# Low parts and masking on GpSimd, wider value products and a bf16 sum in a hybrid attention layer

## The chip, the cores and the metric

The kernel runs on one core of one Trainium2 chip. The metric is the device time of one launch in microseconds (us). Five engines work side by side, each in the order of its own instructions: TensorE (PE, with its weight loads as PEld), VectorE (DVE), ScalarE (ACT), GpSimd (POOL) and SyncE (SP), which issues most DMAs.

## The reference

One decoder layer on x of 2048 rows by 1024 columns. The rows are normalised and modulated, one projection gives the inputs of two attentions of 8 heads of 64 each, both are gated, put side by side, projected again, normalised and added to x. The change lies in the first attention (A), the "forgetting" one, with a causal mask and a bias from a cumulative sum `cum` of log gates:

```python
s = jnp.einsum('bhqd,bhkd->bhqk', qb, kh, preferred_element_type=jnp.float32) * scale
s = s + cb[..., None] - cum[:, :, None, :]
causal = key_pos[None, :] <= q_pos[:, None]
s = jnp.where(causal, s, -jnp.inf)
p = jax.nn.softmax(s, axis=-1)
return jnp.einsum('bhqk,bhkd->bhqd', p.astype(vh.dtype), vh)
...
y = jnp.concatenate([oa, ob], axis=-1) @ w_out[l]
x = x + gate[:, None, :] * rms_norm(y, g_post[l])
```

All of it is in float32.

## The kernel before

float32 products are made of float16 ones: each operand is split into a high part (rounded to float16) and a low part (what is left), and high x high, high x low and low x high are summed in PSUM.

After a start and the second attention (to about 460 us) comes attention A, 8 heads of 20 steps. A step (`Step`, L1331) holds two blocks of 128 keys (b) against a chunk of 512 queries (ci); u is the block of 128 queries in the chunk. `scores` (L1341) makes the scores transposed, keys on partitions, in one two-bank PSUM tile `st`: two products a block (L1349, L1350), of 512, 384, 256 or 128 columns, since blocks above the diagonal are left out. For the 4 blocks on the diagonal of each chunk a third product adds the mask, an identity times a bf16 matrix of -1e30 (L1352). A step is thus 1024, 896 or 384 columns wide; the last two are the diagonal ones. `exp32` (L1354) takes the exponential on ACT into float32 `p32`; `high` (L1358) rounds it to float16 on ACT; `low` (L1362) subtracts on DVE. `pv` (L1365) multiplies with the values: for each key block and u it runs three products with their own weight loads (L1373 high x (64 high value columns and a column of ones), L1375 high x 64 low value columns, L1376 low x 65), all into 65 columns a u of one PSUM tile `po`. The column of ones gives the softmax denominator. After the last step of a chunk DVE takes the reciprocal (L1380) and one product (L1382) into `ona`, and `o_store` (L283) splits and stores it: the high part on ACT, the low part on DVE (L291), DMAs on SP. `po` has one buffer, so the next chunk's first product waits for L1382. `p32` and `ph` have three.

The order is written out by hand in one loop over the steps (L1671). In step s: `exp32(s)`; delayed actions (`tick`); `low(s-1)`; half of the step's other work; `high(s)`; `scores(s+1)`; `tick`; `pv(s-2)`; the other half. The other work is what fills PE: units of three products of the next heads' projections (L351), and products for the row maxima (L1300), each followed on DVE by a maximum (L1303 or L1305) that frees its PSUM bank. `rows` (L1308) turns maxima into limbs by small DVE instructions (L1317 to L1320). Weights for later heads are loaded by POOL (`w_load`, L221), their largest element goes out and back through HBM (L230, L235), and they are split (L267, L273); gate products are stored by POOL (L394) after DVE's product (L392). The gate of the output is summed on DVE (`gate_use`, L1237), and the output weights are split in the last two heads (L1443).

The output projection follows, 16 tiles of 128 rows (`Out`, L1462), begun in the last head. Each tile is scaled by a power of two near the root of its sum of squares: ACT sums each partition (L1510), PE adds over partitions by a float32 product with a matrix of ones (`scale_`, L1514).

Of the kernel before, what the change touches and what calls it, by code (L numbers as in the profile page):

```python
# [24 lines left out]
CH = 512  # L25
# [4 lines left out]
NEG = -1.0e30  # L30
# [5 lines left out]
XM, XR, VW = 66, 69, 129  # L36
# [7 lines left out]
def hybrid_layer(  # L44
# [17 lines left out]
    V, A, G, PE, SP = nc.vector, nc.scalar, nc.gpsimd, nc.tensor, nc.sync  # L62
# [12 lines left out]
    const = ctx.enter_context(tc.tile_pool(name="const", bufs=1))  # L75
# [7 lines left out]
    def sm(n, tag):  # L83
        return small.tile([P, n], F32, tag=tag, name=tag)
# [69 lines left out]
    Shp = const.tile([P, KT], F32, name="Shp")  # L154

    ident = const.tile([P, P], F32, name="ident")
    identb = const.tile([P, P], BF16, name="identb")
    identh = const.tile([P, P], F16, name="identh")
    dmaskT = const.tile([P, P], BF16, name="dmaskT")
    lift = const.tile([P, 1], F32, name="lift")  # L160
    pfl = const.tile([P, 1], F32, name="pfl")
    csum = const.tile([P, 8, NB], F32, name="csum")
# [2 lines left out]
    ones = const.tile([P, P], F32, name="ones")  # L165
# [297 lines left out]
    start = ExitStack()  # L463
    st = start.enter_context(tc.tile_pool(name="start", bufs=1, reuse_waits="tile"))
    wad = start.enter_context(tc.tile_pool(name="wad", bufs=8, reuse_waits="tile"))
    with tc.manual_schedule():
# [23 lines left out]
            w_load(key, pieces(key))  # L490
        G.dma_start(snk[:], sinks[0].partition_broadcast(P))
        G.dma_start(bfg[:], b_fgate[0].partition_broadcast(P))
        V.tensor_copy(identb[:], ident[:])
        V.tensor_copy(identh[:], ident[:])
        PE.transpose(bk[0][:, :P], rows[:], ident[:])
        cols = st.tile([P, 40], F32, name="cols")
# [41 lines left out]
        zero = st.tile([P, P], F32, name="zero")  # L538
# [4 lines left out]
        dm32t = st.tile([P, P], F32, name="dm32t")  # L543

        G.affine_select(dm32t[:], zero[:], [[1, P]], ALU.is_ge, NEG, base=0, channel_multiplier=-1)

        G.affine_select(triu[:], ones[:], [[1, P]], ALU.is_ge, 0.0, base=0, channel_multiplier=-1)

# [33 lines left out]
        A.activation(dmaskT[:], dm32t[:], AF.Copy)  # L582

        def col8(name):
            return st.tile([P, KT], F32, name=name)
# [745 lines left out]
    class Step:  # L1331
# [9 lines left out]
        def scores(self):  # L1341
            T, ci = Ts[self.hd % 2], self.ci
            self.st = ps_st.tile([P, 2 * CH], F32, tag="st", name="sta")
            for b, u0, o in self.blocks:
                w = CH - u0 * P
                kb_ = slice(b * P, (b + 1) * P)
                qc = slice(ci * CH + u0 * P, (ci + 1) * CH)
                diag = b >= 4 * ci
                PE.matmul(self.st[:, o:o + w], T[:, 3, kb_], T[:, 1, qc], start=True, stop=False)  # L1349
                PE.matmul(self.st[:, o:o + w], T[0:XR, 2, kb_], T[0:XR, 0, qc], start=False, stop=not diag)  # L1350
                if diag:
                    PE.matmul(self.st[:, o:o + P], identb[:], dmaskT[:], start=False, stop=True)  # L1352

        def exp32(self):  # L1354
            self.p32 = fxp.tile([P, 2 * CH], F32, tag="p32", name="p32")
            A.activation(self.p32[:, :self.w], self.st[:, :self.w], AF.Exp, scale=scl[f"qk{self.hd}"][:], bias=lift[:])  # L1356

        def high(self):  # L1358
            self.ph = fxh.tile([P, 2, 2 * CH], F16, tag="ph", name="pha")
            A.activation(self.ph[:, 0, :self.w], self.p32[:, :self.w], AF.Copy)  # L1360

        def low(self):  # L1362
            V.tensor_tensor(self.ph[:, 1, :self.w], self.p32[:, :self.w], self.ph[:, 0, :self.w], op=ALU.subtract)  # L1363

        def pv(self):  # L1365
            hd, ph = self.hd, self.ph
            if self.first:
                self.po_[0] = ps_po.tile([P, 4, 65], F32, tag="po", name="poa")
            po = self.po_[0]
            for n, (b, u0, o) in enumerate(self.blocks):  # L1370
                for u in range(u0, 4):
                    pq = slice(o + (u - u0) * P, o + (u - u0 + 1) * P)
                    PE.matmul(po[:, u, :], ph[:, 0, pq], vt[:, b, hd, 0:65],  # L1373
                              start=(self.first and n == 0 and u == 0), stop=False)
                    PE.matmul(po[:, u, 0:64], ph[:, 0, pq], vt[:, b, hd, 65:VW], start=False, stop=False)  # L1375
                    PE.matmul(po[:, u, :], ph[:, 1, pq], vt[:, b, hd, 0:65], start=False,  # L1376
                              stop=(self.last and n == len(self.blocks) - 1))
            if self.last:
                rinv = sm(4, "a_ri")
                V.reciprocal(rinv[:], po[:, :, 64])  # L1380
                on = op_.tile([P, 4, 64], F32, tag="ona", name="ona")
                V.tensor_tensor(on[:], po[:, :, 0:64], rinv[:].unsqueeze(2).broadcast_to([P, 4, 64]), op=ALU.mult)  # L1382
# [79 lines left out]
    class Out:  # L1462
# [24 lines left out]
        def turn(self, lag):  # L1487
# [6 lines left out]
            self.sc = sm(1, "w_pw")  # L1494
            hi, lo = self.hl[:, 0], self.hl[:, 1]
            gs = sm(1, "w_mx")

            def gate():
                if self.t < 4:
# [11 lines left out]

            def scale_():
                pg = bk[bank()][:, 0:1]
                PE.matmul(pg, ones[:], gs[:], start=True, stop=True)  # L1514
# [269 lines left out]
```

## Time and profile before

| | |
|---|---|
| time, median of 3 runs | 1157.74 us (1156.0 to 1158.17) |
| time of the profiled execution | 1157.8 us |
| its span, first to last instruction | 1156.1 us |
| PE busy | 1116.8 us (97%) |
| DVE busy | 930.5 us (80%) |
| ACT busy | 661.4 us (57%) |
| POOL busy | 207.5 us (18%) |
| mean granted PE clock | 0.996 |

How to read it: a row of a group gives line, engine, operation, what it writes and reads, shape and count, then the busy time in us and the mean in ns of one, then the idle time of the engine just before these instructions and what ended it. A row of the timeline gives start and length in us, engine, line and operation. A row of waits gives who waited, for whom, the total in us, the times and the longest. Matmuls overlap in PE's pipe, so their lengths add up to more than their time.

### The profile page before, as it was taken

The numbers are of one execution on the slowest core, as the hardware profiler recorded it, in microseconds if no ns is written. First come the engines' busy times: TensorE is split into PE (matmuls) and PEld (weight loads), VectorE is DVE, ScalarE is ACT, GpSimd is POOL, SyncE is SP. The second block draws the span as 40 slices with busy tenths as digits, with TensorE's granted clock in tenths as the row PEclk, the third lists the DMA queues.
The fourth block names the chain that finished last, engine by engine and source line by source line (L and its number), as shares of the span: only waits on it lengthen the run. The fifth ranks groups of instructions, "written<-read, shape, count | busy, mean of one in ns | idle before, by whom it ended". The sixth has DMA issues, their size and how long they took to land. (4 is left out here: it accounts for less than half of the span.)

```text
span 1156.1 us, 25291 instructions
## 1 busy us (share of the span) xinstructions
PE 1116.8 (97%) x9869; PEld 656.3 (57%) x9869; DVE 930.5 (80%) x2137; ACT 661.4 (57%) x1150; POOL 207.5 (18%) x332
## 2 busy tenths in 40 slices
PE   5899999999999999999999999999999999999997
PEld 2475544577765866555555555555555555544444
DVE  7877468987888568788988899888888887878885
ACT  2876344654555421666757666666776778534332
POOL 1122134554556530010010110001000000000000
PEclk9899999999999999999999999999999999999999
DMA  9943355433243232442344342123311337686743
GB/s 333 336 116 72 87 78 96 97 63 90 52 92 88 58 87 58 73 108 29 80 64 87 84 67 70 38 49 76 45 43 34 91 101 206 140 225 197 199 135 109
DMA packets 123476, 120.10 MB, mean 104 GB/s; under 512 B 64948, under 2 KB 100828, under 8 KB 123356
## 3 DMA queue, kind: packets, MB, share of 16 engines
q1 hardware_dynamic: 112088, 85.69, 27.6%
q0 software_dynamic: 10832, 32.50, 13.5%
q8 instruction: 77, 1.26, 0.6%
q14 instruction: 43, 0.35, 0.1%
q10 hardware_dynamic: 436, 0.28, 0.1%
HBM read 64.75 MB, written 25.18 MB: 78 GB/s over the span
## 5 line engine op out<-in xcount | busy, mean ns | idle before, releaser
L1356 ACT ACTIVATE p<-sta,lift,scl_qk 128x1024 f32<-128x1024 f32 (+2 forms) x160 | 172.0, 1075 | 131.6 <-PE sta L1350 82.6
L351 PE MATMUL bk<-hT,wh_qk 128*128 128x512 f16 x768 | 194.7, 378 | 0.0
L1363 DVE TENSOR_TENSOR pha<-p,pha 128x1024 f16<-128x1024 f32 (+2 forms) x160 | 169.1, 1057 | 0.2 <-ACT pha L1360 0.2
L1303 DVE TENSOR_REDUCE a_m<-bk 128x1 f32<-128x512 f32 x192 | 130.4, 686 | 45.8 <-PE bk L1300 44.8
L1576 PE MATMUL bk<-wohl,oz 128*128 128x512 f16 x744 | 165.3, 379 | 1.1 <-DVE oz L1525 0.7
L1360 ACT ACTIVATE pha<-p 128x1024 f16<-128x1024 f32 (+2 forms) x160 | 148.1, 926 | 5.9 <-PE poa L1376 1.2
L1576 PEld LDWEIGHTS <-oz 128*128 128x128 f16 x744 | 71.9, 99 | 82.8 <-DVE oz L1525 1.8
L1376 PE MATMUL poa<-vt,pha 128*128 128x65 f16 x1088 | 116.1, 192 | 1.4 <-DVE pha L1363 1.2
L1373 PE MATMUL poa<-vt,pha 128*128 128x65 f16 x1088 | 116.6, 193 | 0.8 <-DVE ona L1382 0.7
L1375 PE MATMUL poa<-vt,pha 128*128 128x64 f16 x1088 | 116.6, 194 | 0.0
L351 PEld LDWEIGHTS <-wh_qk 128*128 128x128 f16 x768 | 72.1, 97 | 74.4 <-issue 2.1
L1349 PE MATMUL sta<-T 128*128 128x512 f16 (+1 forms) x320 | 110.9, 346 | 2.8 <-ACT p L1356 2.7
L1300 PE MATMUL bk<-T 66*128 66x512 f16 (+2 forms) x320 | 109.7, 348 | 2.4 <-DVE a_m L1303 1.9
L1373 PEld LDWEIGHTS <-pha 128*128 128x128 f16 x1088 | 101.5, 96 | 15.5 <-DVE ona L1382 1.9
L1350 PE MATMUL sta<-T 69*128 69x512 f16 (+1 forms) x320 | 109.8, 348 | 0.0
L1375 PEld LDWEIGHTS <-pha 128*128 128x128 f16 x1088 | 100.9, 97 | 11.4
L1376 PEld LDWEIGHTS <-pha 128*128 128x128 f16 x1088 | 100.8, 99 | 1.8 <-DVE pha L1363 1.7
L351 PE MATMUL bk<-hT,wh_za 128*128 128x512 f16 x384 | 99.7, 378 | 0.0
L369 PE MATMUL bk<-wh_va,hT 128*128 128x256 f16 x768 | 91.9, 273 | 0.0
L351 PE MATMUL bk<-hT,wh_zb 128*128 128x512 f16 x384 | 91.6, 379 | 0.2 <-DVE qc L754 0.2
L351 PE MATMUL bk<-hT,wh_qb 128*128 128x512 f16 x384 | 91.2, 379 | 0.0
L369 PEld LDWEIGHTS <-hT 128*128 128x128 f16 x768 | 73.3, 98 | 12.2 <-issue 2.1
(459 smaller groups left out, 1919.7 us busy)
## 6 DMA issues: line engine op xcount, KB each, us to landing
hT<-in_x_dram SPq DMA_DIRECT2D x20, 512.0 KB
wa<-in_w_ada_dram SPq DMA_DIRECT2D x16, 512.0 KB
z_d<-tz POOLq DMA_DIRECT2D x32, 256.0 KB, 3.0
T<-z_d SPq DMA_DIRECT2D x16, 512.0 KB
T<-stq SPq DMA_DIRECT2D x62, 128.0 KB
out_dram<-hT SPq DMA_DIRECT2D x15, 512.0 KB
xt<-in_x_dram SPq DMA_DIRECT2D x12, 512.0 KB
qs<-qf SPq DMA_DIRECT2D x80, 64.0 KB
```

Of the source, the lines that this page charges most:

```text
L351: PE.matmul(ps, whl[:, a, k, :], hT[ci][:, b, k, :], start=(k == 0 and n == 0), stop=(k == KT - 1 and n == 2))
L369: PE.matmul(ps[:, (u % 2) * 2 * P:(u % 2 + 1) * 2 * P], hT[ci][:, a, k, u * P:(u + 1) * P], wv[p][:, b, k, :], start=(k == 0 and n == 0), ...
L1303: V.tensor_reduce(m3[:, u, pc:pc + 1], mx[:, :w], axis=AX.X, op=ALU.max)
L1349: PE.matmul(self.st[:, o:o + w], T[:, 3, kb_], T[:, 1, qc], start=True, stop=False)
L1350: PE.matmul(self.st[:, o:o + w], T[0:XR, 2, kb_], T[0:XR, 0, qc], start=False, stop=not diag)
L1356: A.activation(self.p32[:, :self.w], self.st[:, :self.w], AF.Exp, scale=scl[f"qk{self.hd}"][:], bias=lift[:])
L1360: A.activation(self.ph[:, 0, :self.w], self.p32[:, :self.w], AF.Copy)
L1363: V.tensor_tensor(self.ph[:, 1, :self.w], self.p32[:, :self.w], self.ph[:, 0, :self.w], op=ALU.subtract)
L1373: PE.matmul(po[:, u, :], ph[:, 0, pq], vt[:, b, hd, 0:65], start=(self.first and n == 0 and u == 0), stop=False)
L1375: PE.matmul(po[:, u, 0:64], ph[:, 0, pq], vt[:, b, hd, 65:VW], start=False, stop=False)
L1376: PE.matmul(po[:, u, :], ph[:, 1, pq], vt[:, b, hd, 0:65], start=False, stop=(self.last and n == len(self.blocks) - 1))
L1576: PE.matmul(py, self.hl[:, i, k, :], w_slot(8 * j + k)[:, cc], start=(k == 0 and m_ == 0), stop=(k == KT - 1 and m_ == 2))
```

## The change

Four things change in attention A and one in the output projection.

- The mask products and their constants go. Where a step's blocks are diagonal, POOL zeroes the masked part of `p32` after the exponential (an `affine_select` in place over the first 128 columns of both blocks). `high` and `low` read `p32` after it.
- `low` runs on POOL.
- For u below 3 the two products with the high part become one of 129 columns, (64 high values, ones, 64 low values). For u = 3 there is no room in the bank, and the three products stay.
- The evacuation adds the two halves: a reciprocal, a copy, a sum, a product for u = 3, and a product from SBUF.
- The sum of the tiles' squares takes the upper 16 bits of both operands as bfloat16.

```diff
                 PE.matmul(self.st[:, o:o + w], T[:, 3, kb_], T[:, 1, qc], start=True, stop=False)
-                PE.matmul(self.st[:, o:o + w], T[0:XR, 2, kb_], T[0:XR, 0, qc], start=False, stop=not diag)
-                if diag:
-                    PE.matmul(self.st[:, o:o + P], identb[:], dmaskT[:], start=False, stop=True)
+                PE.matmul(self.st[:, o:o + w], T[0:XR, 2, kb_], T[0:XR, 0, qc], start=False, stop=True)
...
             A.activation(self.p32[:, :self.w], self.st[:, :self.w], AF.Exp, scale=scl[f"qk{self.hd}"][:], bias=lift[:])
+            b, u0, o = self.blocks[1]
+            if b >= 4 * self.ci:
+                d = self.p32[:, 0:2 * o].rearrange("p (a c) -> p a c", a=2)[:, :, 0:P]
+                G.affine_select(d, d, [[0, 2], [1, P]], ALU.is_ge, 0.0, base=0, channel_multiplier=-1)
...
-            V.tensor_tensor(self.ph[:, 1, :self.w], self.p32[:, :self.w], self.ph[:, 0, :self.w], op=ALU.subtract)
+            G.tensor_tensor(self.ph[:, 1, :self.w], self.p32[:, :self.w], self.ph[:, 0, :self.w], op=ALU.subtract)
...
-                self.po_[0] = ps_po.tile([P, 4, 65], F32, tag="po", name="poa")
-            po = self.po_[0]
+                self.po_[0] = ps_po.tile([P, CH], F32, tag="po", name="poa")
+            whole = self.po_[0]
+            po = [whole[:, VW * u:VW * u + (VW if u < 3 else 65)] for u in range(4)]
...
-                    PE.matmul(po[:, u, :], ph[:, 0, pq], vt[:, b, hd, 0:65],
+                    PE.matmul(po[u], ph[:, 0, pq], vt[:, b, hd, 0:VW if u < 3 else 65],
                               start=(self.first and n == 0 and u == 0), stop=False)
-                    PE.matmul(po[:, u, 0:64], ph[:, 0, pq], vt[:, b, hd, 65:VW], start=False, stop=False)
-                    PE.matmul(po[:, u, :], ph[:, 1, pq], vt[:, b, hd, 0:65], start=False,
+                    if u == 3:
+                        PE.matmul(po[u][:, 0:64], ph[:, 0, pq], vt[:, b, hd, 65:VW], start=False, stop=False)
+                    PE.matmul(po[u][:, 0:65], ph[:, 1, pq], vt[:, b, hd, 0:65], start=False,
...
-                V.reciprocal(rinv[:], po[:, :, 64])
+                V.reciprocal(rinv[:], whole[:, 64:3 * VW + 65:VW])
                 on = op_.tile([P, 4, 64], F32, tag="ona", name="ona")
-                V.tensor_tensor(on[:], po[:, :, 0:64], rinv[:].unsqueeze(2).broadcast_to([P, 4, 64]), op=ALU.mult)
+                p3 = whole[:, 0:3 * VW].rearrange("p (u c) -> p u c", u=3)
+                V.tensor_copy(on[:, 0:3], p3[:, :, 65:VW])
+                V.tensor_tensor(on[:, 0:3], p3[:, :, 0:64], on[:, 0:3], op=ALU.add)
+                V.tensor_scalar(on[:, 3], po[3][:, 0:64], rinv[:, 3:4], None, op0=ALU.mult)
+                V.tensor_tensor(on[:, 0:3], on[:, 0:3], rinv[:, 0:3].unsqueeze(2).broadcast_to([P, 3, 64]), op=ALU.mult)
...
+            gs1 = gs[:].bitcast(BF16)[:, 1:2]
...
-                PE.matmul(pg, ones[:], gs[:], start=True, stop=True)
+                PE.matmul(pg, ones[:].bitcast(BF16).rearrange("p (n two) -> p two n", two=2)[:, 1], gs1,
+                          start=True, stop=True)
```

At the start the bf16 identity (a copy on DVE), the transposed mask (a select on POOL) and its conversion to bf16 (on ACT) go. Line numbers of the changed kernel differ from those of before by up to 11.

POOL in attention A before, in the second head (gw are the gate rows, wr the raw weights, mx_d and mxr the largest elements out and back, z_d the gate products):

```order
L394 DMA z_d<-tz 128x512
L1231 DMA gw_6936<-in_w_ada_dram 128x1024
L394 DMA z_d<-tz 128x512
L221 DMA wr_qk_7244<-in_w_in_dram 128x8x64 x2
L221 DMA wr_za_7312<-in_w_in_dram 128x8x128
```

The same stretch's beginning in the changed kernel (L1350 is the zeroing, L1357 the low part, p is `p32`):

```order
L392 DMA z_d<-tz 128x512
L1357 TENSOR_TENSOR pha<-p_6760,pha 128x1024
L1357 TENSOR_TENSOR pha<-p_6805,pha 128x1024
L1224 DMA gw_6900<-in_w_ada_dram 128x1024
L1357 TENSOR_TENSOR pha<-p_6858,pha 128x1024
L1350 AFFINE_SELECT p_6949<-p_6949 128x2x128
L1357 TENSOR_TENSOR pha<-p_6902,pha 128x1024
L1350 AFFINE_SELECT p_7005<-p_7005 128x2x128
L1357 TENSOR_TENSOR pha<-p_6949,pha 128x896
```

Between two DMA issues now stand low parts, and a step's zeroing stands ahead of the low part of the step before it. A low part stands behind a store that waits for DVE.

PE before, where the scores of a diagonal step end and value products begin (T are the stacked queries and keys):

```order
L1350 MATMUL sta<-T_6056 128x384
L1352 LDWEIGHTS identb
L1352 MATMUL sta<-dmaskT,identb 128x128
L1373 LDWEIGHTS pha
L1373 MATMUL poa<-vt,pha 128x65
L1375 LDWEIGHTS pha
L1375 MATMUL poa<-vt,pha 128x64
L1376 LDWEIGHTS pha
L1376 MATMUL poa<-vt,pha 128x65
```

And such a place in the changed kernel:

```order
L1342 MATMUL sta<-T_6047 128x384
L1368 LDWEIGHTS pha
L1368 MATMUL poa<-vt,pha 128x129
L1372 LDWEIGHTS pha
L1372 MATMUL poa<-vt,pha 128x65
```

The mask product with its weight load is gone, and two of the three weight loads and products remain.

DVE at the end of a chunk, before (a_ri is the reciprocal, a_m are maxima):

```order
L1363 TENSOR_TENSOR pha<-p_7799,pha 128x1024
L1305 ISA bk_136,a_m<-bk_136,cmask 128x128
L1305 ISA a_m 128x1
L1380 RECIPROCAL a_ri<-poa 128x4
L1382 TENSOR_TENSOR ona<-poa,a_ri 128x256
L1303 TENSOR_REDUCE a_m<-bk_138 128x1
```

And in the changed kernel:

```order
L1376 RECIPROCAL a_ri<-poa 128x4
L1379 COPY ona<-poa 128x192
L1380 TENSOR_TENSOR ona<-poa,ona 128x192
L1381 TENSOR_SCALAR ona<-poa,a_ri 128x64
L1382 TENSOR_TENSOR ona<-ona,a_ri 128x192
```

The low part is no longer ahead of the evacuation; of its five instructions four read the bank, and the last reads SBUF alone.

More of the change, by code (lines that the diff above doesn't have):

```diff
@@ L156, in hybrid_layer @@
     ident = const.tile([P, P], F32, name="ident")
-    identb = const.tile([P, P], BF16, name="identb")
     identh = const.tile([P, P], F16, name="identh")
-    dmaskT = const.tile([P, P], BF16, name="dmaskT")
     lift = const.tile([P, 1], F32, name="lift")
@@ L492, in hybrid_layer @@
         G.dma_start(bfg[:], b_fgate[0].partition_broadcast(P))
-        V.tensor_copy(identb[:], ident[:])
         V.tensor_copy(identh[:], ident[:])
@@ L542, in hybrid_layer @@
         G.affine_select(dm32[:], zero[:], [[-1, P]], ALU.is_ge, NEG, base=0, channel_multiplier=1)
-        dm32t = st.tile([P, P], F32, name="dm32t")
-        G.affine_select(dm32t[:], zero[:], [[1, P]], ALU.is_ge, NEG, base=0, channel_multiplier=-1)
         G.affine_select(triu[:], ones[:], [[1, P]], ALU.is_ge, 0.0, base=0, channel_multiplier=-1)
@@ L581, in hybrid_layer @@
         A.activation(dmask[:], dm32[:], AF.Copy)
-        A.activation(dmaskT[:], dm32t[:], AF.Copy)
         def col8(name):
@@ L1347, in scores @@
                 qc = slice(ci * CH + u0 * P, (ci + 1) * CH)
-                diag = b >= 4 * ci
                 PE.matmul(self.st[:, o:o + w], T[:, 3, kb_], T[:, 1, qc], start=True, stop=False)
-                PE.matmul(self.st[:, o:o + w], T[0:XR, 2, kb_], T[0:XR, 0, qc], start=False, stop=not diag)
-                if diag:
-                    PE.matmul(self.st[:, o:o + P], identb[:], dmaskT[:], start=False, stop=True)
+                PE.matmul(self.st[:, o:o + w], T[0:XR, 2, kb_], T[0:XR, 0, qc], start=False, stop=True)
         def exp32(self):
```

## The prediction

> **What bounds the kernel now.** I read the page's totals first, then the busy time by stretch, then the timeline of TensorE.
>
> ```profile
> span 1156.1 us, 25291 instructions
> PE 1116.8 (97%) x9869; PEld 656.3 (57%) x9869; DVE 930.5 (80%) x2137; ACT 661.4 (57%) x1150; POOL 207.5 (18%) x332
> 462.00:1001.00 539.00, 530.96 (x5503) 309.34 (x5502) 465.76 (x1011) 380.13 (x465) 35.55 (x57) 1.00 0.34 76
> 1001.00:1156.00 155.00, 147.09 (x725) 71.10 (x723) 119.01 (x304) 51.95 (x98) 0.00 (x0) 0.99 0.63 175
> ```
>
> The first line is the span; around it lie 1.7 us, since the profiled execution took 1157.8 us, which is the median of the runs to within 0.1 us. The last two rows give length, then the busy time of PE, PEld, DVE, ACT and POOL, the granted clock, and DMA. The causal attention runs from 462 to 1001 us; nearly all of the change lies there. PE is busy for 531 of its 539 us at full clock; behind it only the output projection is left, where PE is full again. DVE, at 466 of 539, is next; POOL is almost free. So a nanosecond taken from PE comes out of the time, and work taken off DVE does not, unless DVE makes PE wait. A busy figure for PE overlaps in its pipe, so I price products by the distance from one start to the next:
>
> ```profile
> 562.34 0.19 PE L1373 MATMUL poa<-vt,pha 128*128 128x65 f16 x1
> ...
> 563.05 0.19 PE L1376 MATMUL poa<-vt,pha 128*128 128x65 f16 x1
> 563.08 0.38 PE L351 MATMUL bk<-hT,wh_za 128*128 128x512 f16 x1
> ...
> 614.17 0.22 PE L1352 MATMUL sta<-dmaskT,identb 128*128 128x128 bf16 x1
> 614.23 0.19 PE L1373 MATMUL poa<-vt,pha 128*128 128x65 f16 x1
> 614.26 0.19 PE L1375 MATMUL poa<-vt,pha 128*128 128x64 f16 x1
> 614.29 0.19 PE L1376 MATMUL poa<-vt,pha 128*128 128x65 f16 x1
> ...
> 83.70 0.87 PE L795 MATMUL bk<-wh_vb,hT 128*128 128x136 f16 x12
> 84.41 0.81 PE L351 MATMUL bk<-hT,wh_zb 128*128 128x512 f16 x3
> ...
> 1045.11 0.28 PE L1514 MATMUL bk<-w_mx,ones 128*128 128x1 f32 x2
> 1045.25 0.59 PE L1576 MATMUL bk<-wohl,oz 128*128 128x512 f16 x2
> ```
>
> Between 562.34 and 563.08 stand 24 value products of 64 or 65 columns, 30.8 ns each, every one with its own weights. Twelve products of 136 columns take 0.71 us, 59 ns each. A mask product of 128 columns takes 60 ns, a product of the tiles' squares (two passes) 140 ns. PE's pace thus goes by columns, not by instructions.
>
> **Value products.** Of the 1088 triples (65, 64, 65 columns), the 768 with query block u below 3 become a pair (129 and 65). A triple costs 3 x 30.8 = 92.5 ns, a pair 59 (the 136-column row) + 30.8 = 89.8 ns: 768 x 2.7 ns = **2.1 us less**. The ends: nothing, if 129 columns cost twice 30.8 ns; 23.7 us, if a product's price did not depend on its columns, which the 136-column row rules out.
>
> The Trainium skill, "TensorE: Matmul & The Clock Gate", section "Back-to-back issue gap", says that a stream of weight load and product pairs is spaced at about 81 ns for 128 columns. This trace has 59 and 60 ns in such streams, so it disagrees; the rule stays as a rival below, since it would turn the merge into a loss.
>
> **Mask products.** 128 go (L1352), at 60 ns: **7.7 us less**. **Squares:** 16 times 140 ns become one pass of a column, at most one small product (30.8 ns): 16 x 0.11 = **1.8 us less**. At the start a select like L547's below (0.3 us) and two conversions go too; PE waits for its weights to land there, so I cost them at nothing:
>
> ```profile
> PE pm L514 <- DMA wa<-in_w_ada_dram: 4.9, 3, 2.0
> ```
>
> **Low parts.** 160 DVE subtractions and the weight of what replaces them:
>
> ```profile
> L1363 DVE TENSOR_TENSOR pha<-p,pha 128x1024 f16<-128x1024 f32 x96 | 116.8, 1217 | 0.2 <-ACT pha L1360 0.2
> L1363 DVE TENSOR_TENSOR pha<-p,pha 128x896 f16<-128x896 f32 x32 | 34.7, 1083 | 0.0
> L1363 DVE TENSOR_TENSOR pha<-p,pha 128x384 f16<-128x384 f32 x32 | 17.6, 550 | 0.0
> L547 POOL TENSOR_SCALAR_AFFINE_SELECT triu<-ones 128x128 f32<-128x128 f32 x1 | 0.3, 298 | 0.0
> 190.92 0.65 POOL L932 TENSOR_SCALAR_AFFINE_SELECT ptb<-fold 128x512 f16<-128x512 f16 x1
> 191.51 0.64 POOL L934 TENSOR_SCALAR_AFFINE_SELECT ptb<-fold 128x512 f16<-128x512 f16 x1
> 192.10 0.63 POOL L932 TENSOR_SCALAR_AFFINE_SELECT ptb<-fold 128x512 f16<-128x512 f16 x1
> 192.69 0.63 POOL L934 TENSOR_SCALAR_AFFINE_SELECT ptb<-fold 128x512 f16<-128x512 f16 x1
> 190.96 2.92 DVE L765 TENSOR_TENSOR qc<-qc,qs 128x512 f32<-128x512 f32 x1
> ```
>
> DVE loses 169.1 us. No large POOL subtraction is in the trace. POOL's selects give 0.30 us for 128 and 0.63 us for 512 elements: 0.86 ns an element plus 0.19 us. The low end for a 1024-wide low part is one such pass, 1.07 us; the high end in reach of the rows is two, one an input, 1.96 us. I take the **high end**, since the instruction has two inputs. The 139,264 elements of 160 low parts are then 241 + 30 = 271 us; 64 new selects of 2 x 128 elements at 0.41 us are 26 us; with the 35.6 us that POOL has, it is busy for 332 of 539 us, 62%.
>
> The Trainium skill, "GPSIMD Engine Reference", section "Elementwise — side-by-side cycle accounting", measures 4497 ns for 2048 elements of an addition, so my estimate by that page is 2.25 us for 1024. POOL would be at 68%, and the sum the same.
>
> Is a low part late for PE? ACT ends its high part at 607.48, DVE did the low part at 610.03 only, being in order, and PE uses it at 614.29:
>
> ```profile
> 606.42 1.06 ACT L1360 ACTIVATE pha<-p 128x1024 f16<-128x1024 f32 x1
> 610.03 1.22 DVE L1363 TENSOR_TENSOR pha<-p,pha 128x1024 f16<-128x1024 f32 x1
> PE poa L1376 <- DVE pha L1363: 1.2, 2, 0.6
> PEld L1373 <- DVE ona L1382: 1.9, 3, 0.9
> PE bk L1300 <- DVE a_m L1303: 1.7, 4, 0.7
> ACT p L1356 <- PE sta L1352: 44.3, 41, 4.6
> ```
>
> POOL has 6.8 us for 1.96. A low part may now stand behind a z_d store, whose issue (0.55 us) waits for DVE's 0.68 us product at about the old place of the low part: 610.03 + 0.68 + 0.55 + 1.96 = 613.2, still before 614.29. The 16 stores may cost PE from nothing to 1 us each (16 us); I take **1 us more** in all. PE's 1.2 us of waiting for low parts goes: **1.2 us less**. What queues behind a low part on POOL are those stores and the loads of later weights and gate rows, all asked for several steps before they are used.
>
> **Zeroing.** A high part now waits for a select, 0.41 us after its exponential. ACT's last row above is the cover: in these steps it sat idle for 44.3 us over 41 times, 1.1 us each, until the next scores came. Behind the high part on ACT stands the next exponential, which waits for those scores. I cost it at nothing; without the cover it is 64 x 0.41 = 26 us.
>
> **Evacuation.** Where one reciprocal (0.18 us) and one product (0.42 us) read the bank, now a reciprocal, a copy, a sum and a product do, and a fifth instruction reads SBUF:
>
> ```profile
> L1382 DVE TENSOR_TENSOR ona<-poa,a_ri 128x256 f32<-128x256 f32 x32 | 13.6, 424 | 1.1
> L1380 DVE RECIPROCAL a_ri<-poa 128x4 f32<-128x4 f32 x32 | 5.7, 177 | 5.3 <-PE poa L1376 4.5 <-PE bk L1300 0.7
> ```
>
> Between these rows an element costs 0.98 ns, so 192 elements take 0.36 and 64 take 0.24 us. The bank is held for 0.18 + 0.36 + 0.36 + 0.24 = 1.14 us, 0.54 more, and DVE works 0.9 us more in each of 32 (29 us). PE waits for this bank three times now; each of 31 may add from nothing to 0.54 us (16.7 us). I take five: **2.7 us more**.
>
> **The lock.** The L765 row is the one that speaks against the change: its like next to it takes 0.69 us, and it took 2.92, ending just behind four POOL selects in a row. A DVE instruction with two inputs in SBUF stands still while POOL runs. These have such inputs in the attention:
>
> ```profile
> L291 DVE TENSOR_TENSOR oh<-ona,oh 128x256 f16<-128x256 f32 x24 | 10.0, 418 | 0.0
> L1237 DVE SCALAR_TENSOR_TENSOR gacc<-gw,sil,gacc 128x1024 f32<-128x1024 f32 x7 | 8.9, 1277 | 0.0
> L273 DVE SCALAR_TENSOR_TENSOR wh_qk<-wr_qk,w_sw,wh_qk 128x512 f16<-128x512 f32 x12 | 8.9, 745 | 0.0
> L1443 DVE SCALAR_TENSOR_TENSOR wohl<-hT,wsc,wohl 128x512 f16<-128x512 f32 x8 | 6.0, 749 | 4.8 <-ACT wohl L1442 4.7
> L1319 DVE SCALAR_TENSOR_TENSOR a_mr<-lq,a_m 128x4 f32<-128x4 f16 x29 | 4.7, 163 | 1.0
> ```
>
> With 6 more of L273, 8 of L1443 and the 32 new products from SBUF they are 126. At 62% of the time they meet POOL, half a low part before its end: 126 x 0.62 x 1.0 = 78 us. DVE then has 466 - 169 + 29 + 78 = 404 us, under the 466 with which PE waits for it for 1.7 us. I cost the lock at **nothing** in the forecast.
>
> **Sum.** 1157.8 - 2.1 - 7.7 - 1.8 - 1.2 + 1.0 + 2.7 = 1148.7: **1149 us**, with its own range 1143 to 1154.
>
> **Rivals.** A measurement of this kernel can tell about 0.2% (2.3 us) from no change.
> - *The lock makes DVE the bound* (slower). Behind a store or a weight load POOL falls back and then runs selects and low parts one after the other, as in the L765 row, where the wait was 2.2 us and not half an instruction. PE needs DVE's maxima to get its banks back. At 95% busy DVE can do 512 us in this stage; (512 - 326) / 126 = 1.5 us of mean wait is where it decides. At 1.7 us it has 540 us of work, the stage takes 569, and the time is 1157.8 + 30 - 1.5 = 1186. For it: 126 meetings and POOL in runs. Against: POOL starts a low part as soon as the high part ends and is idle for a third of a step. 28%.
> - *POOL is the bound* (slower): 62 us are taken, so 139,264 elements fit in 539 us only up to 3.5 us for each 1024. At 4.2 us POOL has 633 us: 1157.8 + 94 = 1252. No row is near it. 7%.
> - *The gain is eaten by the bank of the output*: every evacuation adds its 0.54 us: 1148.7 - 2.7 + 16.7 = 1163 at the most; with two thirds, 1157. For it: three waits now. Against: the other 28 have time. 12%, of which 2 still end faster.
> - *A 129-column product costs 81 ns*: 768 x (81 + 30.8 - 92.5) = 14.8 us more in place of 2.1 less: 1166. The skill's page named above says so; the 60 ns rows speak against it. 3%.
> That the change does not do what it says is excluded by the order of its instructions.
>
> **How the numbers follow.** The forecast has 50%. Faster: 50 + 2 = 52%; within 0.2%: 10%; slower: 28 + 7 + 3 = 38%. The range goes from the forecast's low end, 1143, to 1190, which takes in most of the lock's rival and leaves out POOL as the bound.
>
> **What would show it.** In the changed profile: value pairs at 90 ns; no 128-column mask products; a 1024-wide low part of about 2 us on POOL, ended before PE's first low product; DVE's busy time in the attention near 400 us, of which the excess of L291, L273 and the maxima's limbs over the means above is the lock. I am wrong if PE's idle time in the attention grows past 15 us, with banks waiting for DVE as its cause, or if a low part takes over 3 us.

## Result and the profile after

The changed kernel takes 1196.74 us in the median of four runs (1193.76 to 1198.54), the kernel before 1157.74 (1156.0 to 1158.17): a ratio of 1.0337 [1.0316, 1.0358], some 39 us **slower**. The forecast was 1149, its range ended at 1190. The profiled execution took 1195.97 us.

First the totals of the changed kernel's page, with its account of the chain that ended last:

```profile
span 1193.8 us, 23715 instructions
PE 1117.5 (94%) x8957; PEld 647.1 (54%) x8957; DVE 942.7 (79%) x2072; ACT 661.8 (55%) x1149; POOL 530.3 (44%) x555
...
PE 59%; DVE 24%; DMA 5%; ACT 5%; issue 4%; POOL 1%; SPq 0%; ACTq 0%; DVEq 0%; POOLq 0%
```

PE has 912 products fewer and is busy for as long as before (1116.8). In the chain DVE now holds 24%; POOL, which took over the low parts, holds 1%. The attention now runs from 462 to 1038 us (before: to 1001), and what follows it takes as long as before (155.8 us against 155.1 by the two spans). So the table by stretch for this stage (length; busy time of PE, PEld, DVE, ACT, POOL; clock; DMA):

```profile
462.00:1038.00 576.00, 530.39 (x4596) 300.16 (x4594) 477.59 (x941) 379.25 (x462) 357.87 (x281) 0.99 0.30 70
```

PE is idle for 576 - 530.4 = 45.6 us, where it was 8.0. Its busy time has not shrunk, in part because 6.8 us of it go to a halved clock (last section). DVE is busy for 83%, less than before (86%). POOL is busy for 62%, the share that was forecast, but of a longer stage: 358 us in place of 332. What PE waits for in this stage (what waits, for whom; us in total, times, longest):

```profile
PE bk L1293 <- DVE a_m L1296: 13.1, 10, 3.3
PE sta L1341 <- ACT p L1346: 10.5, 13, 2.3
PE bk L1250 <- DVE lk L1270: 5.3, 5, 2.3
PE bk L1293 <- DVE stq L1066: 3.9, 3, 1.6
PE poa L1368 <- DVE ona L1381: 3.2, 3, 1.7
PE bk L1293 <- DVE a_m L1298: 3.0, 4, 1.1
PE bk L1578 <- DVE oz L1527: 2.8, 1, 2.8
...
PEld L1372 <- POOL pha L1357: 0.5, 2, 0.3
```

Some 34 us of PE's waiting are for DVE (about 5 before): for maxima that free a bank (13.1, where before had 1.7), for limbs, for the output. Another 10.5 are for scores behind ScalarE (2.7 before). The low parts on POOL, the last row, are nearly never late. The costly groups of DVE and POOL in this stage, by shape (busy us, mean ns of one), and last the two rows of the limbs before:

```profile
L1382 DVE TENSOR_TENSOR ona<-ona,a_ri 128x192 f32<-128x192 f32 x31 | 46.6, 1502 | 0.0
L289 DVE TENSOR_TENSOR oh<-ona,oh 128x256 f16<-128x256 f32 x23 | 35.6, 1548 | 0.0
L1310 DVE TENSOR_SCALAR lq<-a_m 128x4 f16<-128x4 f32 x29 | 32.1, 1105 | 1.0
L1313 DVE TENSOR_SCALAR lq<-a_mr 128x4 f16<-128x4 f32 x29 | 20.9, 720 | 1.0
L1230 DVE SCALAR_TENSOR_TENSOR gacc<-gw,sil,gacc 128x1024 f32<-128x1024 f32 x7 | 17.6, 2513 | 0.0
L1380 DVE TENSOR_TENSOR ona<-poa,ona 128x192 f32<-128x192 f32 x31 | 11.1, 358 | 1.1
L1357 POOL TENSOR_TENSOR pha<-p,pha 128x1024 f16<-128x1024 f32 x96 | 206.0, 2153 | 36.7 <-ACT pha L1354 35.8
L1350 POOL TENSOR_SCALAR_AFFINE_SELECT p<-p 128x256 f32<-128x256 f32 x64 | 29.4, 460 | 105.5 <-ACT p L1346 95.8 <-PE bk L1293 4.0 <-PE poa L1372 3.5
...
L1317 DVE TENSOR_SCALAR lq<-a_m 128x4 f16<-128x4 f32 x29 | 4.9, 170 | 1.0
L1320 DVE TENSOR_SCALAR lq<-a_mr 128x4 f16<-128x4 f32 x29 | 4.9, 170 | 1.0
```

A low part of POOL's takes 2.15 us; my estimate from the rows was 1.96. The Trainium skill's figure ("GPSIMD Engine Reference", section "Elementwise — side-by-side cycle accounting") gave an estimate of 2.25; the trace lies between. The DVE rows are the news. The sum out of the bank (L1380) takes 0.36 us; the product of the same size behind it, with both inputs in SBUF (L1382), takes 1.50. The stored output's low part went from 418 to 1548 ns, the limbs (4 elements, one input each) from 170 to 1105 and 720.

How that becomes idle time of PE is seen in the changed kernel's timeline around PE's longest wait (start, duration, engine, line):

```profile
664.67 4.22 POOL L1357 TENSOR_TENSOR pha<-p,pha 128x1024 f16<-128x1024 f32 x2
668.83 1.80 POOL L219 DMA_DIRECT2D wr_qk<-in_w_in_dram  x2
670.65 3.08 POOL L1357 TENSOR_TENSOR pha<-p,pha 128x1024 f16<-128x1024 f32 x1
673.68 0.58 POOL L1224 DMA_DIRECT2D gw<-in_w_ada_dram  x1
...
665.38 6.38 DVE L1230 SCALAR_TENSOR_TENSOR gacc<-gw,sil,gacc 128x1024 f32<-128x1024 f32 x1
671.68 2.88 DVE L289 TENSOR_TENSOR oh<-ona,oh 128x256 f16<-128x256 f32 x1
674.48 1.28 DVE L1296 TENSOR_REDUCE a_m<-bk 128x1 f32<-128x512 f32 x2
...
671.04 0.22 PE L1368 MATMUL poa<-vt,pha 128*128 128x129 f16 x1
671.10 0.19 PE L1372 MATMUL poa<-vt,pha 128*128 128x65 f16 x1
671.13 0.22 PE L1368 MATMUL poa<-vt,pha 128*128 128x129 f16 x1
...
675.21 0.41 PE L1293 MATMUL bk<-T 66*128 66x512 f16 x1 [3.29 <-DVE a_m L1296]
```

DVE begins an instruction of 1.28 us (its mean before) at 665.38 while POOL runs two low parts and issues two weight loads. It ends at 671.76, 6.38 us later; POOL's third low part takes 3.08 in place of 2.15, as it would if POOL waited for DVE at its start. Then L289 waits behind that third low part and the issue of gate rows that follows it. For 9.2 us DVE's queue does two instructions of 1.7 us together, and the maxima stand behind them. PE gets its bank 3.29 us late. The pair of value products in the PE rows (671.04 to 671.13) takes 90 ns, as forecast.

### The profile page after: what moved, and what is told of

Same layout as the page of the kernel before. It is cut to its first block, busy times and chain, and to the rows that moved or that the text cites. A ratio compares the mean times of both kernels' runs of the same rounds, so it can differ in the third digit from the quotient of the medians.

```text
span 1193.8 us, 23715 instructions
## 1 busy us (share of the span) xinstructions
PE 1117.5 (94%) x8957; PEld 647.1 (54%) x8957; DVE 942.7 (79%) x2072; ACT 661.8 (55%) x1149; POOL 530.3 (44%) x555
## 4 chain that ended last, share of the span: by engine, by line
PE 59%; DVE 24%; DMA 5%; ACT 5%; issue 4%; POOL 1%; SPq 0%; ACTq 0%; DVEq 0%; POOLq 0%
PE bk L349 20%; PE bk L1578 12%; PE bk L367 7%; PE sta L1341 3%; DVE ona L1382 3%; PE sta L1342 3%; PE bk L1293 3%; DVE a_m L1296 3%; PE poa L1368 2%; DMA wa<-in_w_ada_dram 2%; PE poa L1372 2%; PE pss L882 1%; DVE oh L289 1%; PE pob L939 1%; ACT p L1346 1%
## 5 line engine op out<-in xcount | busy, mean ns | idle before, releaser
L1357 POOL TENSOR_TENSOR pha<-p,pha 128x1024 f16<-128x1024 f32 (+2 forms) x160 | 295.7, 1859 | 36.8 <-ACT pha L1354 35.8
L1341 PE MATMUL sta<-T 128*128 128x512 f16 (+1 forms) x320 | 110.2, 349 | 10.8 <-ACT p L1346 10.5
L1368 PE MATMUL poa<-vt,pha 128*128 128x129 f16 (+1 forms) x1088 | 114.3, 214 | 3.2 <-DVE ona L1381 3.2
L1372 PE MATMUL poa<-vt,pha 128*128 128x65 f16 x1088 | 114.6, 194 | 0.1
L1368 PEld LDWEIGHTS <-pha 128*128 128x128 f16 x1088 | 99.8, 98 | 17.7 <-DVE ona L1381 3.7
L1372 PEld LDWEIGHTS <-pha 128*128 128x128 f16 x1088 | 97.4, 99 | 14.4 <-POOL pha L1357 0.5
L1350 POOL TENSOR_SCALAR_AFFINE_SELECT p<-p 128x256 f32<-128x256 f32 x64 | 29.4, 460 | 105.5 <-ACT p L1346 95.8
L1298 DVE CUSTOM_DVE_ANT_0 bk<-bk,cmask 128x128 f32<-128x128 f32 (+3 forms) x128 | 62.0, 497 | 11.5 <-PE bk L1293 11.0
```

Source lines behind the costliest of these rows:

```text
L1357: G.tensor_tensor(self.ph[:, 1, :self.w], self.p32[:, :self.w], self.ph[:, 0, :self.w], op=ALU.subtract)
L1368: PE.matmul(po[u], ph[:, 0, pq], vt[:, b, hd, 0:VW if u < 3 else 65], start=(self.first and n == 0 and u == 0), stop=False)
L1372: PE.matmul(po[u][:, 0:65], ph[:, 1, pq], vt[:, b, hd, 0:65], start=False, stop=(self.last and n == len(self.blocks) - 1))
```

## The experiments

Each ratio is to the kernel before on the same chip, whose median lay between 1155.1 and 1155.7 us in these runs; 1% is 11.6 us.

**1. The low parts back on DVE, all else changed.**

```diff
-            G.tensor_tensor(self.ph[:, 1, :self.w], self.p32[:, :self.w], self.ph[:, 0, :self.w], op=ALU.subtract)
+            V.tensor_tensor(self.ph[:, 1, :self.w], self.p32[:, :self.w], self.ph[:, 0, :self.w], op=ALU.subtract)
```

> The changed kernel with the low part back on DVE; the zeroing on POOL, the 129-column products, the evacuation and the bf16 sum stay. The lock theory (DVE's instructions with two inputs in SBUF stand still while POOL runs a low part, and PE then waits for the banks that DVE frees) expects 1146 to 1153 us, with the low product on banks gone: PE waits for DVE under 6 us in the attention. The zeroing theory (ACT waits for POOL's select, so scores come late) expects 1170 us or more, with ACT still waiting for the select for 30 us or more and PE for ACT for 8 us or more. The evacuation theory (five DVE instructions in place of two hold the bank) also expects 1170 or more, with PE waiting for the evacuation.

Measured: 1157.28 us, ratio 1.0017 [1.0007, 1.0026], between the ranges and 4 us above that of the lock. Of the 39 us 37 are gone with one line, and DVE's rows are free again, though it has 170 us more to do:

```profile
L1382 DVE TENSOR_TENSOR ona<-ona,a_ri 128x192 f32<-128x192 f32 x32 | 11.7, 367 | 0.0
L289 DVE TENSOR_TENSOR oh<-ona,oh 128x256 f16<-128x256 f32 x24 | 10.0, 418 | 0.0
```

The low parts' place is what costs; but the other four edits, forecast to bring 9 us, bring none. In this kernel's attention PE still waits 9.1 us for DVE (under 6 was expected) and 7.9 for scores, and the halved clock takes 3.4.

**2. The low parts on POOL, nothing else changed** (the same line, in the kernel before).

> The kernel before with the low part on POOL and nothing else changed. The lock theory expects 1185 to 1215 us: all of the loss and none of what PE saved. The zeroing and evacuation theories expect 1152 to 1160 us, since neither is in this kernel.

Measured: 1172.78 us, 1.0145 [1.0130, 1.0160]: 17 us slower, between what the two theories expected. DVE loses its 169 us of low parts, PE gains nothing.

**3. The merged value products, their evacuation and the squares, on the kernel before.**

> The kernel before with the 129-column products, their evacuation and the bf16 sum of squares alone; mask on PE and low part on DVE as before. The lock theory expects 1152 to 1157 us (2.1 + 1.8 us saved on PE, up to 2.7 lost at the evacuation). The evacuation theory expects 1165 us or more. If a pair costs as much as the skill's 81 ns would make it, 1166.

Measured: 1159.23 us, 1.0024 [1.0014, 1.0034]. Forecast for these edits: 2.1 and 1.8 us less, 2.7 more, so 1.2 less; measured 2.8 more, above the expected 1152 to 1157. PE waits longer for the output bank than in the rows of before (its weight loads 1.9 us in 3 times, its products 0.7 once):

```profile
PEld L1374 <- DVE ona L1387: 5.2, 5, 1.9
...
PE poa L1374 <- DVE ona L1387: 3.7, 5, 1.7
```

That is 3 us more. Another 3.4 us of this profiled execution, the slowest of nine, go to the halved clock.

**4. The zeroing on POOL, with no mask products, on the kernel before.**

```diff
-                if diag:
-                    PE.matmul(self.st[:, o:o + P], identb[:], dmaskT[:], start=False, stop=True)
...
+                G.affine_select(d, d, [[0, 2], [1, P]], ALU.is_ge, 0.0, base=0, channel_multiplier=-1)
```

> The kernel before with the zeroing of masked probabilities on POOL in place of PE's mask products, and nothing else. The lock theory expects 1149 to 1154 us (7.7 us saved on PE; 64 selects of 0.46 us lock little). The zeroing theory expects 1165 us or more, ACT waiting for POOL for 30 us or more.

Measured: 1155.88 us, 1.0003 [0.9993, 1.0013]: neither. PE has the mask products less to do, 7.7 us by the forecast's price, and the time is the same. The waits of this kernel in the attention:

```profile
ACT p L1353 <- PE sta L1349: 92.2, 94, 4.5
...
ACT pha L1361 <- POOL p L1357: 45.0, 52, 3.8
...
PE sta L1348 <- ACT p L1353: 7.3, 12, 1.0
```

and those of the kernel before:

```profile
ACT p L1356 <- PE sta L1350: 82.6, 74, 2.8
ACT p L1356 <- PE sta L1352: 44.3, 41, 4.6
PE sta L1349 <- ACT p L1356: 2.7, 5, 0.7
```

ACT now waits 45.0 us for selects, 0.87 each; its waits for scores shrink from 126.9 to 92.2, so 35 of the 45 are covered. By the order of the loop the other 10 make the next exponential late, and with it the one bank pair of the scores: PE waits 4.6 us longer there. The halved clock takes another 1.7 us, so some 6 of the 7.7 us are found again.

**5 and 6. Low parts with the merge and the squares; low parts with the zeroing.** The whole is 39 us, the parts alone 16.8 + 2.8 + 0.3 = 20. Which two meet?

> The kernel before with the low parts on GpSimd, the merged value products and the bfloat16 squares; the mask stays on PE. Together the whole change cost about 39 us, the low parts alone 17.4, the merge with the squares 3.9, the zeroing 0.5: some 17 us appear only when parts meet. Theory A (evacuation behind GpSimd): the new product of two inputs from SBUF at the evacuation's end, and the low part of the stored output after it, wait for GpSimd and hold VectorE's maxima up; then this kernel has most of the meeting: 1180 to 1192, and L1382's product takes above 1.2 us here. Theory B (GpSimd's queue shared with the zeroing): the parts only add up here, 1155.4 + 17.4 + 3.9 = 1174 to 1179.

> The kernel before with the low parts and the zeroing on GpSimd; value products and squares as before. Theory A (evacuation behind GpSimd): the parts only add up, 1155.4 + 17.4 + 0.5 = 1171 to 1176. Theory B (GpSimd's queue shared): a low part stands ahead of the next pair's select, so exp's result comes later to the high part, ScalarE's next exp and PE's scores; this kernel has most of the meeting: 1180 to 1192, with PE's waits for scores behind ScalarE above 12 us.

Measured: with the merge 1191.79 us, 1.0303 [1.0275, 1.0331]; with the zeroing 1171.76, 1.0139 [1.0112, 1.0166]. The first pair is 35.0 - 16.8 - 2.8 = 15 us above its sum, the second at its sum. So low parts on POOL meet what came with the merge, and its evacuation holds the slow rows below. The theory of POOL's shared queue falls: with the zeroing PE waits 4.9 us for scores, not above 12. Some 4 us of the 39 appear in neither pair. About half of the 15 us is more halved clock in the profiled executions (last section). The second pair has nearly as much of it, and PE is idle there for less than its parts add up to. The rows of the first pair:

```profile
L1388 DVE TENSOR_TENSOR ona<-ona,a_ri 128x192 f32<-128x192 f32 x31 | 40.8, 1317 | 0.0
L291 DVE TENSOR_TENSOR oh<-ona,oh 128x256 f16<-128x256 f32 x23 | 37.7, 1639 | 0.4 <-ACT oh L295 0.4
```

**7. The two waiting products given to POOL as well.** The evacuation's last product and the stored output's low part leave DVE; everything else as changed.

```diff
-                V.tensor_tensor(on[:, 0:3], on[:, 0:3], rinv[:, 0:3].unsqueeze(2).broadcast_to([P, 3, 64]), op=ALU.mult)
+                G.tensor_tensor(on[:, 0:3], on[:, 0:3], rinv[:, 0:3].unsqueeze(2).broadcast_to([P, 3, 64]), op=ALU.mult)
...
-            V.tensor_tensor(oh[:, :, 1], on, oh[:, :, 0], op=ALU.subtract)
+            (G if eng is SP else V).tensor_tensor(oh[:, :, 1], on, oh[:, :, 0], op=ALU.subtract)
```

> The changed kernel with two operations of VectorE given to GpSimd as well: the evacuation's last product and the low part of the stored outputs (both with two inputs from SBUF, 83 us of VectorE's time in the attention, some 55 of it above what they take alone). Theory A (they are slow because GpSimd runs, and PE's banks wait behind them): 1168 to 1185. Theory B (GpSimd's queue is what is late): GpSimd gets 40 us more, so 1195 to 1210.

Measured: 1177.31 us, 1.0195 [1.0174, 1.0217]: 16 us come back although POOL has more to do, and PE's waits for DVE in the attention fall from 34 to 24 us. DVE and POOL (third and fifth busy time) have 443 and 387 us of 563 now:

```profile
462.00:1025.00 563.00, 530.49 (x4593) 301.39 (x4592) 443.41 (x888) 376.75 (x463) 386.94 (x335) 0.98 0.31 72
```

The limbs still wait (1342 ns for L1310's); what share of the rest is theirs, no run separates.

**8, 9 and 10. The lock by itself.** The kernel before, low parts on DVE, with idle work of POOL behind each low part in two halves: the same subtraction again, memsets, or copies.

```diff
+            for c in (slice(0, h), slice(h, self.w)):
+                G.tensor_tensor(dum[:, :h], self.p32[:, c], self.ph[:, 0, c], op=ALU.subtract)
```

(with `G.memset(dum[:, :h], 0.0)` and `G.tensor_copy(dum[:, :h], self.p32[:, c])` in its place).

> The kernel before, unchanged in all it computes, with one addition: behind VectorE's low part GpSimd subtracts the same two tiles once more, in two halves, into a tile that nothing reads. No result of GpSimd's is waited for, but p32 and ph come free only after it. The lock (VectorE's instructions with two inputs from SBUF wait while GpSimd runs): the low parts themselves on VectorE and the limbs' products get slower, at least the 17 us of the low parts alone: 1170 to 1200, with VectorE's 1024-wide low part above 1.6 us on average. The rival (the low part on GpSimd cost time because it is slower and late there): nothing waits for this one: 1154 to 1160.

> The kernel before with two memsets of half the width on GpSimd behind each low part, into a tile that nothing reads, in place of the repeated subtraction that cost 78 us. If any running instruction of GpSimd's holds VectorE up, about as long as it runs: 1175 to 1215. If what holds VectorE up are GpSimd's reads (two inputs from SBUF): 1154 to 1160, with VectorE's 1024-wide low part near 1.06 us as before.

> The kernel before with two idle copies of half the width on GpSimd behind each low part (one input, p32, into a tile that nothing reads), in place of the repeated subtraction (1234.0) or the memsets (1155.4). If any read of GpSimd's from SBUF holds VectorE's two-input instructions up: 1165 to 1205, with the 1024-wide low part on VectorE above 1.25 us. If only an instruction of GpSimd's with two inputs does: 1154 to 1160.

Measured: subtractions 1233.99 us, 1.0673 [1.0655, 1.0692], 34 us above the lock's range; memsets 1155.38, 0.9998 [0.9989, 1.0007]; copies 1163.79, 1.0067 [1.0050, 1.0084], 1.2 us below what I had put for reads. DVE's low part of 1024 elements and the idle instruction of POOL, with the subtractions:

```profile
L1364 DVE TENSOR_TENSOR pha<-p,pha 128x1024 f16<-128x1024 f32 x96 | 161.9, 1686 | 0.2 <-ACT pha L1361 0.2
...
L1367 POOL TENSOR_TENSOR dum<-p,pha 128x512 f16<-128x512 f32 x192 | 284.0, 1479 | 33.3 <-ACT pha L1361 18.9 <-ACT rw L1262 2.4
```

with the memsets:

```profile
L1364 DVE TENSOR_TENSOR pha<-p,pha 128x1024 f16<-128x1024 f32 x96 | 116.7, 1216 | 0.2 <-ACT pha L1361 0.2
...
L1367 POOL MEMSET dum<- 128x512 f16 x192 | 101.5, 528 | 9.2
```

and with the copies:

```profile
L1364 DVE TENSOR_TENSOR pha<-p,pha 128x1024 f16<-128x1024 f32 x96 | 129.2, 1346 | 0.2 <-ACT pha L1361 0.2
...
L1367 POOL CAST dum<-p 128x512 f16<-128x512 f32 x192 | 152.7, 795 | 59.6 <-ACT p L1357 51.4
```

The three have the same instructions on PE, DVE and ACT. POOL's reads hold the low parts up, its writes do not: 1217 ns before, 1216 with memsets, 1346 and 1686 with reads. The limbs are another case: writes slow them a little too, from 170 to 241 and 212 ns with memsets. With the subtractions DVE is busy for 582 of the stage's 610 us, and the time grows by 78:

```profile
462.00:1072.00 610.00, 553.13 (x5483) 316.60 (x5482) 581.92 (x1007) 380.12 (x463) 449.68 (x377) 0.96 0.28 67
```

Not all of the 78 us need be DVE's: the halved clock takes 22 us of the profiled execution, and ACT waits 21.6 us for idle instructions that still hold `p32`; PE waits 4 us longer than before for ACT's exponentials.

The Trainium skill, "SBUF — State Buffer", section "Who interferes with whom", says that a VectorE instruction with two inputs in SBUF contends with GpSimd's reads from it and not with its writes, and that single-input forms like tensor_scalar can contend too, in modes that their operands must allow. These runs agree with the first: 1686 against 1216 ns. The one-input limbs took 1105 ns in the changed kernel; in which mode they ran, no run here shows.

**11. Each low part on POOL as two halves.** Does DVE get in between?

```diff
+            for c in (slice(0, self.w // 2), slice(self.w // 2, self.w)):
+                G.tensor_tensor(self.ph[:, 1, c], self.p32[:, c], self.ph[:, 0, c], op=ALU.subtract)
```

> The changed kernel with each low part on GpSimd as two instructions of half the width; the work is the same, GpSimd pays one instruction's overhead more for each. If a waiting instruction of VectorE's gets in when an instruction of GpSimd's ends, its mean wait about halves: 1172 to 1190, and the 192-element product of the evacuation takes under 1.1 us. If it waits through GpSimd's back-to-back instructions: 1193 to 1205, with the product at 1.4 us or more.

Measured: 1183.26 us, 1.0241 [1.0224, 1.0257], 11 us better than the changed kernel by the ratios, and the mean of the product is still 1354 ns. Neither theory was whole; the 32 single durations of the product (ns, sorted, from the traces) tell why:

```
changed kernel:  16 times 347-360, then 460 665 764 1004 1007 1180 1585 1648 2190 2706 | 3631 4490 4510 4590 5048 5844
low in halves:   16 times 346-386, then 397 428 499 547 598 675 807 844 914 930 | 3934 4764 4776 5006 5335 6264
```

The middle waits shrink with the halves, which fits waits that end with one instruction of POOL's. The six long ones stay: where POOL has low parts queued up, DVE does not get in between them. The longest of the changed kernel (489.1 to 495.0 us) lies beside two low parts, the issue of gate rows and a third low part, which ends at 494.75.

**12. The evacuation straight from the bank, low parts on POOL.** All five operations behind the reciprocal read PSUM.

```diff
+                V.tensor_tensor(on[:, 0:3], p3[:, :, 65:VW], rinv[:, 0:3].unsqueeze(2).broadcast_to([P, 3, 64]), op=ALU.mult)
+                for u in range(3):
+                    V.scalar_tensor_tensor(on[:, u], po[u][:, 0:64], rinv[:, u:u + 1], on[:, u], op0=ALU.mult, op1=ALU.add)
```

> The changed kernel (low parts on GpSimd) with another evacuation: each of its five operations behind the reciprocal reads the bank, none has two inputs from SBUF; the bank is held longer (about 1.6 us in place of 1.14). If the evacuation's last product waits for GpSimd and PE's banks wait behind it: 1178 to 1189, though the bank comes free later. If the shorter hold of the bank counts for more than the wait: 1196 to 1210.

Measured: 1189.82 us, 1.0295 [1.0279, 1.0310], a little above the expected 1189. The new operations take 278 and 357 ns, unheld, and 5 us come back net of the longer hold of the bank. In the profiled executions PE's idle time in the attention falls by 7.2 us, while the halved clock takes 5.1 more. The product's own share is thus 5 us at least; by the sum of the parts the merge with its evacuation is in for 15. What lies between the two figures is not separated.

**13. The squares alone.**

> The kernel before with the bfloat16 squares only. If the terms of the sum are right where nothing stands against them: 1155.4 - 1.8 = 1153.0 to 1154.5. Then the merged value products with their evacuation cost about 5.5 us of what the merge with the squares measured (1159.2 - 1153.6), where the forecast had -2.1 + 2.7. If the squares bring nothing: 1155.0 to 1156.0.

Measured: 1154.37 us, 0.9984 [0.9975, 0.9993]: 1.8 us less, which is the term of the sum. That it fits to the tenth is luck, since the interval goes from 0.8 to 2.9 us.

**14. The zeroing with the high part behind the next exponential, and the squares.**

```diff
             if s:
+                if steps[s - 1].late_high:
+                    steps[s - 1].high()
                 steps[s - 1].low()
...
-            stp_.high()
+            if not stp_.late_high:
+                stp_.high()
```

> The kernel before with the zeroing on GpSimd and the bfloat16 squares, low parts on VectorE; and the high part of a pair with zeroing is issued behind the next pair's exp instead of ahead of it, so that ScalarE does not stand behind GpSimd's select. If the zeroing's gain of 7.7 us was lost because that wait held ScalarE's next exp and with it PE's scores (9.6 us of stalls at the scores with the zeroing alone, 3.8 before): 1146 to 1151. If it was lost elsewhere, or the later high part makes the low part and the value products late: 1152 to 1160.

Measured: 1152.30 us, 0.9969 [0.9958, 0.9980], the only version with the zeroing on POOL that beats the kernel before, by 3.6 us, 1.8 of it the squares'. PE's wait for scores is back near its old 2.7 us:

```profile
PE sta L1349 <- ACT p L1354: 3.2, 6, 0.8
...
PE poa L1375 <- ACT pha L1362: 1.4, 1, 1.4
PE poa L1375 <- DVE ona L1384: 1.4, 2, 1.2
```

Even so the time misses the 1146 to 1151 expected of the loop and lies in the range for a loss elsewhere or late value products. The new order is worth about 2 us against experiment 4, and its attention has no halved clock. So 2 of the mask products' 7.7 us are had; the two last rows (0.7 us at that place before) show some of the rest.

## Why the prediction was wrong, step by step

- **Value products, mask products, squares** (PE's side). The prices are not contradicted: a pair takes 90 ns in the trace, and the squares gave 1.8 us by themselves (experiment 13). No run times a mask product by itself. The rival with 81 ns for 129 columns is out.
- **The low part on POOL**: 2.15 us for 1.96, PE's wait for it 0.5 us. Right enough; that POOL's share came out at the forecast 62% is luck, since both its work and the stage were longer. The rival with POOL as the bound is out.
- **Evacuation, 2.7 us**: mis-sized. The merge and the squares cost 2.8 us together; with 2.1 and 1.8 taken off, the evacuation cost about 6.7. Five waits of PE's were taken and five are in the row of experiment 3, but they make 3 us more than before; the halved clock's 3.4 us, which no term of the sum stood for, come on top.
- **Zeroing at nothing**: failed. The cover was real for 35 of 45 us of ACT's waiting only. I had taken idle time of ACT, summed over the stage, for cover of each single step. The 10 left over lie in a loop of exponential, scores and the next exponential; a changed order of that loop brought about 2 us back (experiment 14), and the rest of the mask products' 7.7 us is explained in part only.
- **"I cost the lock at nothing"**: the step that failed, and with it the forecast. Its first half held: rows of the trace before did show the lock, and 126 meetings were put at 78 us. Measured, from the mean times of the groups above less the free ones, are 31 x 1.14 + 23 x 1.13 + 7 x 1.24 = 70 us for the three large groups on that list and some 13 for the rest of it. But 29 x (0.94 + 0.55) = 43 more went to the single-input limbs, which were not on it, and others were held as well: DVE was busy for 478 us, not the 404 forecast, so the lock took some 150 above the 326 without it. The second half did not hold either: "DVE then has 404 us, under the 466". DVE's total stayed under the bound (478 of 576 us), and PE waited 34 us for it all the same. A busy sum says whether an engine can keep up on average; the lock does not add half a microsecond everywhere, it leaves half of the products alone and stops six for 3.6 to 5.8 us. Behind a stop of that length stand the maxima that free PE's banks.
- **The clock** was no term of the sum, which took full clock throughout, as the attention had before. In the changed kernel's attention 6.8 us are lost to half clock, most of what the 10 us of products that went would have saved.
- **The lock's rival** named the right cause and place and the wrong condition: DVE at 95% and 1.5 us of mean wait. It decided at 83% and, on the 126 of the list, 83 / 126 = 0.7 us. Its 1186 us was 11 us too low, and the range ended 7 us below the result.
- **"I am wrong if PE's idle time in the attention grows past 15 us, with banks waiting for DVE as its cause"**: it grew from 8.0 to 45.6, and 34 of that are waits for DVE.

Shown by runs: the low parts' place costs 37 of the 39 us (1), reads of POOL's slow DVE with no result changed (8 to 10), and taking two held operations from DVE brings 16 us back (7). Argued from the timeline and the waits only: how the single stops turn into PE's waits. Open: how much of the 15 us is the evacuation's last product, and what sets off the halved clock.

## What to carry to other kernels

In this kernel, work that read SBUF on an idle GpSimd was paid for by VectorE's instructions with inputs in SBUF. List those, single-input ones too, and look at what stands behind them in VectorE's queue, not at VectorE's busy share. The merge with its evacuation and the squares cost 3 us, the reading job on GpSimd 17, both together 35: so try edits in pairs before adding up what each does alone. Leaving the job where it was helped most; reading the PSUM bank instead brought 5 us. Idle time covers a delay only in the step where it lies; where an engine's next work comes back to it through another one's, check that loop first.

## What the runs showed of the hardware

A held instruction of VectorE's does not always wait for one instruction of GpSimd's but through several queued ones (5.84 us at most for the product, for 0.35 us of work), and cutting them in halves shortens only the short waits. GpSimd pays as well: its half-width subtraction takes 1479 ns beside VectorE's low parts and 1171 where those are on GpSimd (experiment 11).

PE's clock is halved now and then: right behind the 3.29 us of the timeline above, the changed kernel's table by stretch shows half clock for 3.4 us (the sixth column, not counting the length), where PE's products take nearly twice as long. The attention has 13.6 us of it, about 6.8 us lost; before it had none.

```profile
671.70:675.20 3.50, 0.21 (x7) 0.12 (x4) 3.50 (x4) 1.86 (x2) 3.48 (x3) 1.00 0.38 80
675.40:678.80 3.40, 3.40 (x9) 1.20 (x8) 3.03 (x10) 0.00 (x0) 2.01 (x2) 0.50 0.96 258
```

A long wait is not needed. In experiment 4 half clock begins at 925.8 us, behind four waits of 1.4 us together within 3.4 us, none above 0.65. Nor does more idle time mean more half clock, as PE's idle time in the attention and the time lost to half clock there show (one profiled execution each, the clock read in stretches of 1 us):

| run | idle, us | lost, us |
|---|---|---|
| before | 8.0 | 0 |
| 14, zeroing with the later high part | 11.3 | 0 |
| 4, zeroing | 12.9 | 1.7 |
| 3, merge and squares | 14.1 | 3.4 |
| 1, all but the low parts | 17.6 | 3.4 |
| 2, low parts | 22.6 | 1.7 |
| 6, low parts and zeroing | 22.1 | 12.0 |
| 5, low parts, merge and squares | 36.5 | 13.7 |
| 12, evacuation from the bank | 38.4 | 11.9 |
| the changed kernel | 45.6 | 6.8 |
